# A second buffer for turned tokens, earlier loads, another layout of the norm sums and wide recurrence steps in the SSD units of a hybrid encoder block

## The chip, the core and the metric

The kernel runs on one NeuronCore of a Trainium2 chip, as one launch. The metric is the device time of one execution in microseconds (us); the runs are summed up by their median. The core's engines are TensorE (PE; its weight loads are listed apart as PEld), VectorE (DVE), ScalarE (ACT), GpSimd (POOL) and SyncE (SP), and 16 DMA engines move data between the memory HBM and the on-chip SBUF. TensorE writes to PSUM, a small memory of 8 banks here, which VectorE and ScalarE read.

## The reference

One block on a sequence of 1024 tokens of width 1024. The change lies in the Mamba-2 (SSD) heads: 16 heads of width 64, in two groups, chunks of 128 tokens, both directions.

```python
h = rms_norm(x, norm_mix_pre);  z, xbc, dt_raw, u = split(h @ w_in)
xh, b_ssm, c_ssm = split(silu(conv(xbc)))            # 16 heads of 64; states of 128
# _ssd_scan, once per direction:
scores = einsum("bclgn,bcsgn->bcgls", cc, bc)
y_diag = einsum("bcgrls,bcsgrp->bclgrp", scores[:, :, :, None] * decay, xdt)
states = einsum("bclgn,bcgrl,bclgrp->bcgrpn", bc, decay_to_end, xdt)   # one per chunk
states_in = einsum("bzcgr,bcgrpn->bzgrpn", m, states)                  # decayed sum over earlier chunks
y_off = einsum("bclgn,bcgrpn,bcgrl->bclgrp", cc, states_in, exp(a_cum))
# behind both directions:
y = (y_f + y_b + xh * d_skip) * silu(z)
y_ssd = rms_norm(y, norm_w, per group of 512 channels)
y_s5 = s5_mixer(u)                                   # ends in g * sigmoid(g @ glu_w + glu_b)
x = x + rms_norm(concat(y_ssd, y_s5) @ w_out)
x = x + rms_norm((silu(n @ w_gate) * (n @ w_up)) @ w_down)   # n = rms_norm(x)
```

## The kernel before

The program runs in stages: input projection with the S5 scan (to about 540 us), the SSD units (about 590 to 945 us), the mixing norm, and the feed-forward part (from about 1014 us to the end). All large products are in three float32r terms (high by high, high by low, low by high halves).

**The units.** The work on the 16 heads is cut into eight units of two heads, `unit(q)`, q = 0 to 7; units 0 to 3 are norm group 0, 4 to 7 group 1. They are woven into three other pieces of TensorE work by generators (`fill_with`): the GLU product of the S5 half (line 277, up to about 698 us), the output product of the S5 half (line 1137, `out_s5`) and that of SSD group 0 (line 1137, `out_g0`). A tile scheduler orders each engine's instructions by priorities (`hpri`) and its own costs; the order on each engine is then fixed, and every engine works through its own list in order. SP issues most of the DMAs, and waits in order too.

**One unit.** Four tensors are loaded by `unit_loads(q)`: the two operands `la` and `ra` of the decay exponents (from `na_d` and `rr_d` in HBM) and the tokens `xT`. TensorE turns `xT` (line 871), ScalarE copies the result to `X` (872), VectorE and GpSimd multiply it by the step weights of one direction each to `Xw` (943), and TensorE makes the chunk states from it (956, 28 matmul instructions of 128 columns). The recurrence over chunks stands on VectorE (967): `Sn[step] = Sn[step-1] * cd + state`, six steps with four instructions of 64 columns each, one per direction and head. Then, for each half of the sequence, decays (981 to 989), the masked scores `M` (1002, 1003), the products (1008, 1022) and the sums in `y` (1010 to 1027).

**Its tail.** ScalarE squares `y` (1032 or 1035), VectorE adds the squares to `ssum` (1036), ScalarE and VectorE write `y` as two halves `hl` (1040, 1041), with the tokens ordered by step, and SP stores them to `ch_d` and `cl_d` (1042, 1043). After four units `group_norm` sums `ssum` over the partitions by 16 matmul instructions (1050); in them every weight load reads `ssum` at a distance of 8 elements. The output products load `ch_d` and `cl_d` as `cat` (1127), and `out_g0` adds to partial sums `m` that go through `m_d` (load 1162, sum on VectorE 1166, store 1167; two buffers).

**Before the units**, `dt_prep` makes the step weights `wdt`, the chunk decays `cd`, and the sums' halves `rhl` (858, 859), which GpSimd stores to `rr_d` and `na_d` by eight DMAs (862, 863); `unit_loads(0)` reads them back. `rhl` and `X` share one buffer.

Of the kernel before, what the change touches and what calls it, by code (L numbers as in the profile page):

```python
# [9 lines left out]
F32 = mybir.dt.float32  # L10
F32R = mybir.dt.float32r
I32 = mybir.dt.int32
AF = mybir.ActivationFunctionType
ALU = mybir.AluOpType
PSUM = bass.MemoryType.PSUM
ADD, SUB, MUL = ALU.add, ALU.subtract, ALU.mult
# [116 lines left out]
def hymba_block(ctx, tc, P, out, dbg=None, upto=99):  # L133
# [663 lines left out]
    def dt_prep():  # L797
# [5 lines left out]
        t = ptmp()  # L803
# [30 lines left out]
        t = ptmp()  # L834
# [17 lines left out]
        for d in range(2):  # L852
            pe.matmul(t[:, 128 * d:128 * d + 128], af[:, d].rearrange("p c h -> p (c h)"), (tri_le, tri_ge)[d], start=True, stop=True)
            pe.transpose(t[:, 256 + 128 * d:384 + 128 * d], ln[:, d].rearrange("p c h -> p (c h)"), ident)
        rhl = un.tile([128, 2, 4, 128], F32R, tag="X", name="rhl")
        rh, rl = rhl[:, 0], rhl[:, 1]
        tv = t.rearrange("p (n l) -> p n l", n=4)
        act.copy(rh, tv)
        dve.tensor_tensor(rl, tv, rh.bitcast(F32), op=SUB)
# [71 lines left out]
    def unit(q, ssum):  # L931
        g = q // 4
        with hpri("u1"):
            L, Rr = la[q % 2], ra[q % 2]
            if q not in uts:
                unit_loads(q)
            xT = uts[q]
            X = un.tile([128, 8, 128], F32, tag="X", name="X")
            transposes(X, xT)
            Xw = un.tile([128, 2, 8, 2, 64], F32, tag="Xw", name="Xw")  # L940
            for d in range(2):
                w = wdt[:, :, 16 * d + 2 * q:16 * d + 2 * q + 2].unsqueeze(3).to_broadcast([128, 8, 2, 64])
                pd(f"xw{d}").tensor_tensor(Xw[:, d], X.rearrange("p c (h e) -> p c h e", h=2), w, op=MUL)
            zt = un.tile([128, 1024], F32, tag="zt", name="zt")
            sp.dma_start(zt, z_d[128 * q:128 * q + 128, :])
        yield
        with hpri("u2"):

            Sn = un.tile([128, 2, 7, 128], F32, tag="Sn", name="Sn")
            for s0 in range(0, 7, 2):  # L950
                t = ptmp()
                ns = min(2, 7 - s0)
                for d in range(2):
                    for s in range(ns):
                        c = s0 + s if d == 0 else 7 - s0 - s
                        pe.matmul(t[:, 256 * s + 128 * d:256 * s + 128 * d + 128], Bt[:, c, g, :],  # L956
                                  Xw[:, d, c].rearrange("p h e -> p (h e)"), start=True, stop=True)
                for s in range(ns):
                    st = s0 + s
                    if st == 0:  # L960
                        act.copy(Sn[:, :, 0, :], t[:, 0:256].rearrange("p (d e) -> p d e", d=2))
                        continue
                    for d in range(2):
                        for hh in range(2):
                            es = slice(64 * hh, 64 * hh + 64)
                            o = 256 * s + 128 * d + 64 * hh
                            dve.scalar_tensor_tensor(Sn[:, d, st, es], Sn[:, d, st - 1, es], cd[:, d, st, 2 * q + hh:2 * q + hh + 1],
                                                     t[:, o:o + 64], op0=MUL, op1=ADD)
            if q in KN['cd']:
                conv_silu(*conv_taps(q + 4, None))  # L970
        y = un.tile([128, 1024], F32, tag="yg", name="yg", bufs=2)
        for hf in range(2):
            with hpri("u3"):
                sl = HF[hf]
                rv = Rr[:, 4 * hf:4 * hf + 4, :].rearrange("p c l -> p (c l)")
                Es, EFs = [], []
                for hh in range(2):
                    E = un.tile([128, 2, 512], F32, tag="E", name="E", bufs=2)
                    for d in range(2):
                        xp = ptmp()  # L980
                        pe.matmul(xp, L[:, 4 * d + 2 * hf + hh, :], rv, start=True, stop=False)
                        pe.matmul(xp, idr, neg[:, d].rearrange("p c l -> p (c l)"), start=False, stop=True)
                        act.activation(E[:, d], xp, AF.Exp)
                    Es.append(E)
                for d in range(2):
                    EF = un.tile([128, 512], F32, tag="EF", name="EF", bufs=2)
                    xp = ptmp()
                    pe.matmul(xp, efs[:, d, :], rv, start=True, stop=True)
                    act.activation(EF, xp, AF.Exp)
                    EFs.append(EF)  # L990
                if hf == 1 and q < 7:
                    unit_loads(q + 1)
            yield
            with hpri("u4"):
# [33 lines left out]
            if hf == 0:  # L1028
                yield
        with hpri("u4"):  # L1030
            if q % 4 == 0:
                act.activation(ssum, y, AF.Square)
            else:
                sq = io.tile([128, 1024], F32, tag="io", name="sq")
                act.activation(sq, y, AF.Square)
                pd('ss').tensor_tensor(ssum, ssum, sq, op=ADD)
            hl = un.tile([128, 2, 8, 128], F32R, tag="hl", name="hl")
            w = vec2[:, R_N + q:R_N + q + 1]
            yv = y.rearrange("p (k l) -> p l k", l=8)
            act.activation(hl[:, 0], yv, AF.Copy, scale=w)  # L1040
            dve.scalar_tensor_tensor(hl[:, 1], yv, w, hl.bitcast(F32)[:, 0], op0=MUL, op1=SUB)
            Q[KN["cq"]].dma_start(ch_d[128 * q:128 * q + 128], hl.bitcast(F32)[:, 0])
# [2 lines left out]
    @pri("gn")  # L1045
    def group_norm(g, ssum):
        t = ptmp()
        sv = ssum.rearrange("p (k l) -> p l k", l=8)
        for l in range(8):
            pe.matmul(t[:, l:l + 1], sv[:, l, :], ones[:, 0:1], start=True, stop=True)  # L1050
        rms_scale(t[:, 0:8], rg[:, g, :], 1.0 / 512, 1e-5)
# [917 lines left out]
```

## Time and profile before

| | |
|---|---|
| runs before | median 1693.84 us of 3 (1693.69 to 1709.21) |
| the profiled execution | 1697.36 us, its span on the core 1695.7 us, mean granted TensorE clock 0.963 |
| TensorE, matmul | busy 1557.0 us, 92% of the span |
| VectorE | busy 1252.1 us, 74% |
| ScalarE | busy 728.0 us, 43% |
| GpSimd | busy 537.6 us, 32% |
| DMA | 271.61 MB, 160 GB/s over the span |

The profiled execution is the one that the trace shows; its own time is 0.2% over the median of the runs. A busy share is a mean over stages with different limits. Engines are named by their short names, times are counted from the start of the span, and a line number is one of the kernel before.

### The profile page before, as it was taken

The page shows a single profiled execution, that of the slowest core. Times are in us where ns is not written, and L with a number is a line of the kernel's source. Part 1 is how long each engine was busy: PE and PEld are TensorE (multiplying, and loading weights), DVE is VectorE, ACT ScalarE, POOL GpSimd, SP SyncE. Part 2 cuts the span into 40 slices and gives each one's busy share as a digit, 9 for nine tenths or more (in the row PEclk, how much of TensorE's full clock was granted, in tenths as well). Part 3 has the DMA queues.
Part 4 walks back from the last instruction along what each step waited for, and adds up shares of the span by engine and source line. Part 5 has one row for each costly group of instructions (what it writes and reads, how often), then busy time and mean ns, then how long its engine had stood idle before and what let it go on. Part 6 is the DMA issues. An engine that isn't in the chain of part 4 may idle for free.

```text
span 1695.7 us, 22363 instructions
## 1 busy us (share of the span) xinstructions
PE 1557.0 (92%) x7980; PEld 1270.2 (75%) x7980; DVE 1252.1 (74%) x2022; ACT 728.0 (43%) x1238; POOL 537.6 (32%) x499
## 2 busy tenths in 40 slices
PE   7998999889787879999998997999999999999897
PEld 6777788668675666778787775788888888787686
DVE  7445589999862567887576578788888788669777
ACT  6354632122598445444343277322222232344352
POOL 2111121157121020112111041555555555239512
PEclk9999999989799889999999998999999999999999
DMA  6543343243687748777668892333322221592234
GB/s 182 155 134 107 115 153 124 94 128 98 151 210 191 210 129 273 242 245 244 194 217 267 282 297 72 104 119 122 106 100 94 100 100 56 203 341 71 94 111 175
DMA packets 250003, 271.61 MB, mean 160 GB/s; under 512 B 29387, under 2 KB 190659, under 8 KB 249891
## 3 DMA queue, kind: packets, MB, share of 16 engines
q1 hardware_dynamic: 224515, 215.96, 41.2%
q0 software_dynamic: 12896, 33.83, 6.3%
q10 hardware_dynamic: 12480, 20.39, 3.4%
q8 instruction: 63, 1.03, 0.3%
q14 instruction: 49, 0.40, 0.1%
HBM read 185.23 MB, written 84.84 MB: 159 GB/s over the span
## 4 chain that ended last, share of the span: by engine, by line
PE 39%; DVE 10%; DMA 8%; issue 4%; ACT 3%; POOL 3%; SPq 0%; DVEq 0%; POOLq 0%; ACTq 0%
PE acc L1550 13%; PE ptmp L1550 10%; PE acc L1137 4%; PE ptmp L1856 4%; PE acc L1856 3%; DVE dop L1838 2%; DMA m<-m_d 2%; PE acc L277 1%; PE ptmp L956 1%; POOL wd L1823 1%; DMA m_d<-m 1%; DMA cl_d<-ghl 1%; DVE cacc L724 1%; PE ptmp L1022 1%; DMA graw<-g_d 1%
## 5 line engine op out<-in xcount | busy, mean ns | idle before, releaser
L277 PE MATMUL acc<-hTh,whi 128*128 128x512 f32 (+1 forms) x456 | 179.9, 395 | 8.5 <-ACT whi L267 8.0
L1137 PE MATMUL acc<-ohi,cat 128*128 128x512 f32 x512 | 175.7, 409 | 8.6 <-DMA cat<-ch_d 5.5
L277 PE MATMUL acc<-hTh,wlo 128*128 128x512 f32 (+1 forms) x456 | 179.1, 393 | 2.2 <-POOL wlo L268 2.1
L277 PE MATMUL acc<-hTl,whi 128*128 128x512 f32 (+1 forms) x456 | 179.4, 394 | 0.5 <-DVE hTl L337 0.5
L1533 DVE TENSOR_TENSOR wop<-rawp,wop 128x512 fp32r<-128x512 f32 x120 | 137.7, 1148 | 17.9 <-ACT wop L1532 16.7
L1550 PE MATMUL ptmp<-T,wop 128*128 128x512 f32 x528 | 127.9, 399 | 4.1 <-ACT T L1706 3.7
L1550 PE MATMUL acc<-T,wop 128*128 128x512 f32 x528 | 125.7, 393 | 1.6 <-DVE T L1709 1.5
L1856 PE MATMUL ptmp<-dop 128*128 128x512 f32 x528 | 122.2, 393 | 2.9 <-DVE dop L1838 2.9
L1550 PE MATMUL acc<-B,wop 128*128 128x512 f32 x528 | 124.6, 392 | 0.0
L1137 PEld LDWEIGHTS acc<-ohi,cat 128*128 128x128 f32 x512 | 99.3, 195 | 33.2 <-DVE s L1673 4.4
L1550 PEld LDWEIGHTS ptmp<-T,wop 128*128 128x128 f32 x528 | 101.2, 192 | 27.2 <-ACT T L1706 3.9
L268 POOL TENSOR_TENSOR wlo<-raw,whi 128x1024 fp32r<-128x1024 f32 x20 | 50.3, 2514 | 222.4 <-ACT whi L267 222.4
L1856 PEld LDWEIGHTS ptmp<-dop 128*128 128x128 f32 x528 | 100.2, 190 | 24.2 <-DVE dop L1838 3.2
L1550 PEld LDWEIGHTS acc<-T,wop 128*128 128x128 f32 x528 | 98.8, 188 | 24.9 <-DVE T L1709 3.3
L1550 PEld LDWEIGHTS acc<-B,wop 128*128 128x128 f32 x528 | 99.1, 188 | 21.7 <-DVE B L1709 0.2
L277 PEld LDWEIGHTS acc<-hTh,whi 128*128 128x128 f32 x456 | 87.1, 191 | 27.0 <-ACT whi L267 8.4
L1565 ACT ACTIVATE cg<-cg 128x512 f32<-128x512 f32 x44 | 27.8, 633 | 183.0 <-DVE cg L1563 182.9
L1838 DVE TENSOR_TENSOR dop<-da,dop 128x512 fp32r<-128x512 f32 x77 | 76.9, 999 | 36.7 <-ACT dop L1837 36.7
L1571 POOL TENSOR_TENSOR cg<-cg 128x512 f32<-128x512 f32 x44 | 61.8, 1405 | 130.5 <-DVE cg L1566 129.8
L277 PEld LDWEIGHTS acc<-hTh,wlo 128*128 128x128 f32 x456 | 87.1, 191 | 21.5 <-POOL wlo L268 4.1
L1532 ACT CAST wop<-rawp 128x512 fp32r<-128x512 f32 x120 | 70.2, 615 | 76.7 <-POOL rawp L1507 51.2
L1137 PE MATMUL acc<-olo,cat 128*128 128x512 f32 x256 | 103.1, 403 | 0.0
(362 smaller groups left out, 3566.1 us busy)
## 6 DMA issues: line engine op xcount, KB each, us to landing
ff_d<-cg POOLq DMA_DIRECT2D x77, 256.0 KB, 2.3
da<-ff_d SPq DMA_DIRECT2D x35, 512.0 KB
raw<-in_w_in_dram SPq DMA_DIRECT2D x28, 512.0 KB
cat<-ch_d SPq DMA_DIRECT2D x48, 256.0 KB
cat<-cl_d SPq DMA_DIRECT2D x48, 256.0 KB
wd<-in_w_down_dram SPq DMA_DIRECT2D x44, 256.0 KB
rawp<-in_w_gate_dram SPq DMA_DIRECT2D x10, 1024.0 KB
rawp<-in_w_up_dram SPq DMA_DIRECT2D x10, 1024.0 KB
```

Source lines behind the costliest of these rows:

```text
L268: (pool if ("0" if j < 2 else "A" if j < XBC0 else "X" if j < Z0 else "Z" if j < GL0 else "G" if j < FF0 else "F") in KN['pl'] else dve).t ...
L277: pe.matmul(ps, a[:, k, :], b[:, k, sl], start=(k == 0 and n == 0), stop=(k == 7 and n == 2))
L724: (pool if ct in KN['pc'] and k in KN['pk'] else dve).scalar_tensor_tensor(a[:, d], xp[:, r], w[k], a[:, d], op0=MUL, op1=ADD)
L956: pe.matmul(t[:, 256 * s + 128 * d:256 * s + 128 * d + 128], Bt[:, c, g, :], Xw[:, d, c].rearrange("p h e -> p (h e)"), start=True, stop=True)
L1137: pe.matmul(ps, c[:, a, k % 4, :], b[:, k % 2, :], start=(k == 0 and n == 0), stop=(k == n_ - 1 and n == 2))
L1532: act.copy(t[:, 0], src)
L1533: dve.tensor_tensor(t[:, 1], src, t.bitcast(F32)[:, 0], op=SUB)
L1550: pe.matmul(ps, a[:, ai, k, :], b[:, bi, k, :], start=(k == 0 and q == 0), stop=(k == 3 and q == 2))
L1565: act.activation(cg[:, 0], cg[:, 0], AF.Silu)
L1571: pool.tensor_tensor(dst, a, b, op=op)
L1838: dve.tensor_tensor(t[:, k, 1], src, t.bitcast(F32)[:, k, 0], op=SUB)
L1856: pe.matmul(ps, t[:, 0, a, 128 * j:128 * j + 128], t[:, 1, b, :], start=(q == 0 and n == 0), stop=(q == NP - 1 and n == 2))
```

## The change

Five edits in `dt_prep`, `unit` and `group_norm`:

1. `X` has two buffers of its own tag.
2. `rhl` leaves that tag and takes the buffer of `hl`, which the first unit's tail is the next to use.
3. `unit_loads(q + 1)` is written in the first half of unit q, not in the second.
4. The squares are written by step: the activation reads `y` at a distance of 8 elements, as the one for `hl` does, and writes in a row; `ssum` is then in the order in which `group_norm` loads it.
5. A step of the recurrence is two instructions of 256 columns in the place of four of 64: a product of two SBUF operands (the decays broadcast), and a sum with the state in PSUM.

```diff
--- before.py
+++ after.py
@@ -852,8 +852,8 @@
         for d in range(2):
             pe.matmul(t[:, 128 * d:128 * d + 128], af[:, d].rearrange("p c h -> p (c h)"), (tri_le, tri_ge)[d], start=True, stop=True)
             pe.transpose(t[:, 256 + 128 * d:384 + 128 * d], ln[:, d].rearrange("p c h -> p (c h)"), ident)
-        rhl = un.tile([128, 2, 4, 128], F32R, tag="X", name="rhl")
-        rh, rl = rhl[:, 0], rhl[:, 1]
+        rhl = un.tile([128, 2, 8, 128], F32R, tag="hl", name="rhl")
+        rh, rl = rhl[:, 0, 0:4], rhl[:, 1, 0:4]
         tv = t.rearrange("p (n l) -> p n l", n=4)
         act.copy(rh, tv)
         dve.tensor_tensor(rl, tv, rh.bitcast(F32), op=SUB)
@@ -935,7 +935,7 @@
             if q not in uts:
                 unit_loads(q)
             xT = uts[q]
-            X = un.tile([128, 8, 128], F32, tag="X", name="X")
+            X = un.tile([128, 8, 128], F32, tag="X", name="X", bufs=2)
             transposes(X, xT)
             Xw = un.tile([128, 2, 8, 2, 64], F32, tag="Xw", name="Xw")
             for d in range(2):
@@ -960,12 +960,9 @@
                     if st == 0:
                         act.copy(Sn[:, :, 0, :], t[:, 0:256].rearrange("p (d e) -> p d e", d=2))
                         continue
-                    for d in range(2):
-                        for hh in range(2):
-                            es = slice(64 * hh, 64 * hh + 64)
-                            o = 256 * s + 128 * d + 64 * hh
-                            dve.scalar_tensor_tensor(Sn[:, d, st, es], Sn[:, d, st - 1, es], cd[:, d, st, 2 * q + hh:2 * q + hh + 1],
-                                                     t[:, o:o + 64], op0=MUL, op1=ADD)
+                    hv = [Sn[:, :, i, :].rearrange("p d (h e) -> p d h e", h=2) for i in (st - 1, st)]
+                    dve.tensor_tensor(hv[1], hv[0], cd[:, :, st, 2 * q:2 * q + 2].unsqueeze(3).to_broadcast([128, 2, 2, 64]), op=MUL)
+                    dve.tensor_tensor(hv[1], hv[1], t[:, 256 * s:256 * s + 256].rearrange("p (d h e) -> p d h e", d=2, h=2), op=ADD)
             if q in KN['cd']:
                 conv_silu(*conv_taps(q + 4, None))
         y = un.tile([128, 1024], F32, tag="yg", name="yg", bufs=2)
@@ -988,7 +985,7 @@
                     pe.matmul(xp, efs[:, d, :], rv, start=True, stop=True)
                     act.activation(EF, xp, AF.Exp)
                     EFs.append(EF)
-                if hf == 1 and q < 7:
+                if hf == 0 and q < 7:
                     unit_loads(q + 1)
             yield
             with hpri("u4"):
@@ -1028,15 +1025,16 @@
             if hf == 0:
                 yield
         with hpri("u4"):
+
+            yv = y.rearrange("p (k l) -> p l k", l=8)
             if q % 4 == 0:
-                act.activation(ssum, y, AF.Square)
+                act.activation(ssum.rearrange("p (l k) -> p l k", l=8), yv, AF.Square)
             else:
                 sq = io.tile([128, 1024], F32, tag="io", name="sq")
-                act.activation(sq, y, AF.Square)
+                act.activation(sq.rearrange("p (l k) -> p l k", l=8), yv, AF.Square)
                 pd('ss').tensor_tensor(ssum, ssum, sq, op=ADD)
             hl = un.tile([128, 2, 8, 128], F32R, tag="hl", name="hl")
             w = vec2[:, R_N + q:R_N + q + 1]
-            yv = y.rearrange("p (k l) -> p l k", l=8)
             act.activation(hl[:, 0], yv, AF.Copy, scale=w)
             dve.scalar_tensor_tensor(hl[:, 1], yv, w, hl.bitcast(F32)[:, 0], op0=MUL, op1=SUB)
             Q[KN["cq"]].dma_start(ch_d[128 * q:128 * q + 128], hl.bitcast(F32)[:, 0])
@@ -1045,7 +1043,7 @@
     @pri("gn")
     def group_norm(g, ssum):
         t = ptmp()
-        sv = ssum.rearrange("p (k l) -> p l k", l=8)
+        sv = ssum.rearrange("p (l k) -> p l k", l=8)
         for l in range(8):
             pe.matmul(t[:, l:l + 1], sv[:, l, :], ones[:, 0:1], start=True, stop=True)
         rms_scale(t[:, 0:8], rg[:, g, :], 1.0 / 512, 1e-5)
```

Since a scheduler sets the order, instructions move too. On GpSimd, at the stores of the sums' halves (`rr_d`, `na_d`) that stand ahead of the first unit:

```order
 L908 MEMSET efs 128x256
 L862 DMA rr_d<-rhl 8x16x128
+L943 TENSOR_TENSOR Xw<-X,wdt 128x1024
 L863 DMA na_d<-rhl 2x64x128
 L862 DMA rr_d<-rhl 8x16x128
```

The first unit's product `Xw` on GpSimd moved ahead of seven of the eight stores; it stood behind the last of them. On ScalarE the two copies to `X` of that unit (872) moved likewise, from behind the cast to `rhl` to a place ahead of the copy to `ac` (838), which the step weights and `rhl` need; on VectorE its `Xw` now stands right behind the second half of `rhl`, and on TensorE its 28 matmul instructions of line 956 stand 22 rows of line 277 earlier, with 25 such rows between them and the first of line 981.

On SP in `out_g0`, where `m0` is the partial sum that is loaded, added to and stored (before):

```order
L1099 DMA oraw_8087<-in_w_out_dram 128x2x512
L1127 DMA cat_7818<-cl_d_66 128x4x128
L1167 DMA m_d_67<-m0_7726 128x512
L1099 DMA oraw_8093<-in_w_out_dram 128x2x512
L1127 DMA cat_7888<-ch_d_65 128x4x128
L1162 DMA m0_7796<-m_d_67 128x512
L1167 DMA m_d_67<-m0_7746 128x512
L1127 DMA cat_7888<-cl_d_66 128x4x128
L1127 DMA cat_7926<-ch_d_65 128x4x128
L1127 DMA cat_7926<-cl_d_66 128x4x128
L1167 DMA m_d_67<-m0_7796 128x512
L1162 DMA m0_7816<-m_d_67 128x512
```

and now:

```order
L1097 DMA oraw_7997<-in_w_out_dram 128x2x512
L1165 DMA m_d_67<-m0_7646 128x512
L1125 DMA cat_7804<-ch_d_65 128x4x128
L1125 DMA cat_7804<-cl_d_66 128x4x128
L1125 DMA cat_7842<-ch_d_65 128x4x128
L1165 DMA m_d_67<-m0_7666 128x512
L1160 DMA m0_7712<-m_d_67 128x512
L1125 DMA cat_7842<-cl_d_66 128x4x128
L1125 DMA cat_7862<-ch_d_65 128x4x128
L1160 DMA m0_7732<-m_d_67 128x512
L1125 DMA cat_7862<-cl_d_66 128x4x128
L1165 DMA m_d_67<-m0_7712 128x512
```

The load of the fourth partial sum (7816, now 7732) stood behind the store of the third (7796) and stands ahead of it now (7712).

On SP at the tail of unit 4, where `hl` are the halves of `y` and `cat` what the output product of the S5 half loads (before):

```order
L945 DMA zt_7288<-z_d_62 128x1024
L1042 DMA ch_d_65<-hl_7233 128x1024
L1127 DMA cat_7425<-ch_d_65 128x4x128
L1127 DMA cat_7425<-cl_d_66 128x4x128
L1127 DMA cat_7428<-ch_d_65 128x4x128
L1127 DMA cat_7428<-cl_d_66 128x4x128
L1043 DMA cl_d_66<-hl_7233 128x1024
L1127 DMA cat_7527<-ch_d_65 128x4x128
```

and now:

```order
L945 DMA zt_7228<-z_d_62 128x1024
L1040 DMA ch_d_65<-hl_7173 128x1024
L1041 DMA cl_d_66<-hl_7173 128x1024
L1125 DMA cat_7357<-ch_d_65 128x4x128
L1125 DMA cat_7357<-cl_d_66 128x4x128
L1125 DMA cat_7360<-ch_d_65 128x4x128
L1125 DMA cat_7360<-cl_d_66 128x4x128
L1125 DMA cat_7455<-ch_d_65 128x4x128
```

The store to `cl_d` moved ahead of four loads of `cat`; in unit 5 it did the same. From unit 3 on the loads of `la`, `ra` and `xT` stand at the same places among their neighbours as before, and so do the turns (871), the copies to `X` and the products `Xw`.

## Rows read from the trace of the kernel before

**Rows 1.** The page, part 1: busy time, share of the span, instructions.
```profile
PE 1557.0 (92%) x7980; PEld 1270.2 (75%) x7980; DVE 1252.1 (74%) x2022; ACT 728.0 (43%) x1238; POOL 537.6 (32%) x499
```

**Rows 2.** Waits by engine and line, TensorE, 590 to 1014: total, times, longest.
```profile
PE ptmp L956 <- DVE Xw L943: 18.8, 7, 8.4
```

**Rows 3.** Timeline of TensorE at the first unit: start, us, instruction, idle before.
```profile
613.58 1.19 PE L956 MATMUL ptmp<-Xw,Bt 128*128 128x128 f32 x4 [8.38 <-DVE Xw L943]
615.25 4.55 PE L956 MATMUL ptmp<-Xw,Bt 128*128 128x128 f32 x24 [0.48 <-POOL Xw L943]
...
619.87 0.40 PE L981 MATMUL ptmp<-ra,la 128*128 128x512 f32 x1
```

**Rows 4.** Windows, 606 to 620: length, busy by engine, granted clock, DMA share, GB/s.
```profile
606.00:620.00 14.00, 5.94 (x30) 5.63 (x31) 7.32 (x17) 4.54 (x7) 2.94 (x1) 0.63 0.33 99
```

**Rows 5.** Timeline of ScalarE at the same place.
```profile
611.10 1.07 ACT L872 COPY X<-ptmp 128x512 f32<-128x512 f32 x2 [10.06 <-DMA na_d<-rhl]
```

**Rows 6.** Timeline of GpSimd at the same place (its DMA issues included).
```profile
598.09 0.61 POOL L862 DMA_DIRECT2D rr_d<-rhl  x1 [37.94 <-ACT rhl L858]
...
602.83 0.80 POOL L863 DMA_DIRECT2D na_d<-rhl  x1
612.26 2.94 POOL L943 TENSOR_TENSOR Xw<-X,wdt 128x1024 f32<-128x1024 f32 x1 [8.63 <-ACT X L872]
```

**Rows 7.** Timeline of SyncE's queue at the same place.
```profile
611.09 0.29 SPq L923 DMA_DIRECT2D la<-na_d  x1
```

**Rows 8.** The tensor na_d: its four stores, issue to landing.
```profile
DMA to landing us min/median/max: 4.3/6.4/8.2
```

**Rows 9.** Timeline of TensorE: the group norms, and unit starts after and without one.
```profile
796.11 4.93 PE L956 MATMUL ptmp<-Xw,Bt 128*128 128x128 f32 x28
...
828.18 3.36 PE L956 MATMUL ptmp<-Xw,Bt 128*128 128x128 f32 x28 [1.37 <-DVE Xw L943]
...
946.42 3.75 PE L1050 MATMUL ptmp<-ones,ssum 128*128 128x1 f32 x16
```

**Rows 10.** Windows around the two group norms (columns as in rows 4).
```profile
790.00:802.00 12.00, 11.66 (x54) 10.97 (x54) 6.78 (x20) 2.71 (x5) 4.57 (x2) 0.72 0.93 285
946.00:960.00 14.00, 12.28 (x45) 10.42 (x44) 4.61 (x6) 2.10 (x2) 1.66 (x1) 0.76 0.86 270
```

**Rows 11.** Timeline of VectorE: dependent adds of 256, and the recurrence of unit 0.
```profile
584.61 0.88 DVE L827 SCALAR_TENSOR_TENSOR e<-e,z 128x256 f32<-128x256 f32 x2
...
618.22 3.92 DVE L967 SCALAR_TENSOR_TENSOR Sn<-Sn,cd,ptmp 128x64 f32<-128x64 f32 x20 [0.45 <-PE ptmp L956]
```

**Rows 12.** Groups by line, ScalarE: count, busy us, mean ns, idle before.
```profile
L1040 ACT ACTIVATE hl<-yg,vec 128x1024 fp32r<-128x1024 f32 x8 | 18.2, 2279 | 0.0
...
L1035 ACT ACTIVATE sq<-yg 128x1024 f32<-128x1024 f32 x6 | 6.4, 1060 | 21.8 <-DVE yg L1027 21.8
```

**Rows 13.** The chain that ended last, 870 to 900: start, us, what.
```profile
880.89 2.42 DMA m<-m_d
...
893.66 0.33 SPq L1167
...
894.08 4.67 DMA m<-m_d
```

**Rows 14.** Timeline of VectorE and TensorE at the start of the last unit.
```profile
900.14 1.22 DVE L943 TENSOR_TENSOR Xw<-X,wdt 128x1024 f32<-128x1024 f32 x1
...
901.50 4.99 PE L956 MATMUL ptmp<-Xw,Bt 128*128 128x128 f32 x28 [4.23 <-DVE Xw L943]
```

**Rows 15.** Timeline of GpSimd and VectorE: the two products of a unit side by side.
```profile
747.80 1.92 POOL L943 TENSOR_TENSOR Xw<-X,wdt 128x1024 f32<-128x1024 f32 x1 [8.61 <-ACT X L872]
...
748.08 2.73 DVE L943 TENSOR_TENSOR Xw<-X,wdt 128x1024 f32<-128x1024 f32 x1
```

**Rows 16.** Timeline of SyncE's queue in unit 4.
```profile
833.25 0.39 SPq L1127 DMA_DIRECT2D cat<-ch_d  x1
...
837.57 0.33 SPq L1043 DMA_DIRECT2D cl_d<-hl  x1
```

## The prediction

> **What bounds the kernel now.** I read the page's busy shares first: TensorE is busy for 92% of the span, VectorE for 74%, ScalarE for 43% [rows 1]. So a microsecond is won only where TensorE idles, runs at a low clock, or takes longer over an instruction than the same work takes elsewhere. The change touches the unit stage alone, so the second view is TensorE's waits between 590 and 1014 us. The largest group there is the chunk states waiting for VectorE's `Xw`: 18.8 us in 7 waits, the longest of them 8.4 [rows 2]. The timelines around that longest wait, at the first unit, come third, and the two group norms fourth. [...] Around the norms the clock is 0.72 and 0.76 with a busy TensorE [rows 10], and the norm's one-column instructions take 3.75 us for 16 [rows 9]. All sums are made on the profiled execution's 1697.36 us and carried to the median of the runs by 1693.84/1697.36, 0.2% less. A change of less than 1%, 17 us, can hardly be told from none by a measurement of this kernel.
>
> **First unit.** ScalarE's copies to `X` wait 10.06 us for the last store of `na_d` to land, because `X` takes over `rhl`'s buffer [rows 5]. Edits 1 and 2 end that. What is late next decides the gain. The decay matmuls of line 981 need `la`, which SP issues when `na_d` has landed: at 611.09 [rows 7]. The order shows that this gets later for two reasons. The two copies to `X` (1.07 for both, rows 5) now stand ahead of work that `rhl` needs on ScalarE, and GpSimd's `Xw` stands ahead of seven of the eight stores, whose issues begin at 598.09 and end at 603.63 [rows 6]. `Xw` on GpSimd takes 2.94 in that place [rows 6] and 1.92 elsewhere [rows 15]; I take 2.94. So `na_d` lands at 611.09 + 1.07 + 2.94 = 615.1. The load of `la` is not in the rows; the nearest prices are 2.42 for a load on SP [rows 13] and 4.3 for the fastest store of `na_d` [rows 8]; I take the middle, 3.36. Line 981 then begins at 618.46, against 619.87 now [rows 3]: 1.41 earlier, and two more instructions of line 277 are done by then, 0.23 each from the starts in the trace's order, 0.46. **Term: -1.9.** With 1.92 and 2.42 it is -3.8, with 2.94 and 4.3 -0.9; the last landing, 7.46 behind the issue's end now, may lie between 4.3 and 8.2 [rows 8], which takes the bounds to -7.0 and -0.2. So the wait isn't removed, it moves from `Xw` to `la`: TensorE does its states and the 25 rows of line 277 early, and then stands before line 981 instead. The clock falls there as it does now, and the 2.4 us lost to it (5.74 less 3.36) are not credited.
>
> **Group norms.** The strided weight loads go. Now an instruction takes 3.75/16 = 0.234 us [rows 9]; the nearest row for one with a dense weight load of that size is line 956, 3.36/28 = 0.12 [rows 9]. 16 x 0.114 = 1.8, twice: **-3.6**, all of it on TensorE's own time. Beyond it, the clock at these places: 12 us at 0.72 and 14 us at 0.76 [rows 10] lose 3.4 each against full speed; unit 4's states right behind the first norm take 4.93 for unit 5's 3.36 [rows 9]. In front of the drop stand the norm's instructions, which fill the engine's time with little work; if they are half as long, the drop may be absent or the same. I take half of 6.8: **-3.4**, bounds 0 and -6.8.
>
> **Partial sums.** In `out_g0` the load of the fourth `m` waits in SP's list behind the store of the third: store issued at 893.66, load at 894.08, and 4.67 us until it lands [rows 13], where a load of the same size alone takes 2.42. VectorE's `Xw` of the last unit stands behind that sum and starts at 900.14, and TensorE waits 4.23 for it [rows 14]. The load moves ahead of that store, by one queue entry of 0.4 us and part of the 2.25 that it lands late: **-1.0**, bounds 0 and -4.2.
>
> **What it costs.** Unit 0 shows a step of the recurrence at 3.92/20 = 0.196 us an instruction; 24 of them are 4.7 us a unit. Twelve dependent instructions of 256 columns cost 0.88/2 = 0.44 each by the two at 584.61 [rows 11], together 5.3: +0.6 a unit on VectorE. [...] The squares take 1.06 now; read at a distance of 8 elements, like line 1040, they take 2.28 [rows 12]: +1.22 on ScalarE in each of 8 tails. In all 8 x (0.6 + 1.22) = 14.6 us of work on engines with room; `hl` is written behind it, one unit or more ahead of who reads it. Only at the last unit is no later unit's work left to cover it, where the norm waits for the squares and the output product for `cat`: 0.6 + 1.22 = 1.8, and 0.7 for places in between where TensorE waits for `M`: **+2.5**, bounds 0 and 14.6.
>
> **SP at the tails of units 4 and 5.** The store to `cl_d` is moved ahead of four `cat` loads. SP works in order, and the store waits for VectorE's half of `hl`: it was issued at 837.57, the first `cat` load at 833.25 [rows 16]. With the squares' 1.22 those four loads come up to 4.32 + 1.22 = 5.5 us later. The output products that read them hold two steps of `cat` in advance; this is the cover, and if it is gone, TensorE waits up to 5.5 in each. **+1.0**, bounds 0 and 11.
>
> **At nothing:** the loads of edit 3 and the second `X` from unit 3 on. The order leaves `la`, `ra`, `xT`, the turns and both `Xw` where they were among their neighbours, so the other six waits of rows 2 remain, but for the 1.0 above.
>
> **Sum:** -1.9 - 3.6 - 3.4 - 1.0 + 2.5 + 1.0 = -6.4, so 1691.0 for the profiled execution and **1687.4** as a median. With the terms' bounds, of which not all fall on one side, this case lies between 1681 and 1692.
>
> **Rivals.**
> *The stall is gone and the clock stays up.* If `la` lands before TensorE has done its 25 rows of line 277, the first unit gives 8.38 + 0.48 + 2.4 = 11.3, and with the whole 6.8 of the norms: -11.3 - 3.6 - 6.8 - 1.0 + 2.5 + 1.0 = -19.2, 1674.7. For it: the wait for `X` is the only one that the trace shows there. Against it: `na_d` lands late even now, and two things are put ahead of it.
>
> *The layout and the new home do next to nothing.* The first unit gains 0.2, the clock falls as before: -0.2 - 3.6 - 1.0 + 2.5 + 1.0 = -1.3, 1692.5. Against it: the slower norm instructions have no other visible reason than their stride.
>
> *Slower: the `cl_d` store ahead of the `cat` loads.* If the loads are not covered in units 1, 4 and 5, where an output product runs, each costs 5.5: 16.5 + 2.5 - 9.9 = +9.1, 1702.9. It decides from the point where a `cat` load lands after TensorE has finished the step before it. For it: a `cat` buffer has little depth, and TensorE hardly idles there now, so every wait would be new. Against it: two steps in advance are more than 5.5 us.
>
> *VectorE behind GpSimd.* The side-by-side products show 2.73 for VectorE's `Xw` [rows 15] against 1.22 alone [rows 14]. The recurrence's new product reads two SBUF operands too, 48 times in all; the old form read PSUM. GpSimd is busy for 32% [rows 1]; 48 x 0.32 x 1.5 (the 2.73 less 1.22) = 23 us more on VectorE, and with half of it on the path -6.4 + 11.5 = +5.1, 1698.9. [...] Against its size: after `Xw`, GpSimd has little to do while the states are made.
>
> **How the numbers follow.** Chances: the forecast 0.50, the next-to-nothing rival 0.22, the full gain 0.10, the `cat` loads 0.13, GpSimd 0.05. The range runs from 1675 to 1700: it leaves out part of the full gain and most of the `cat` case, which has a tail on both sides. Faster by over 1% (under 1676.9) is most of the full gain and the forecast's lower tail, 0.09; slower by over 1% (over 1710.8) needs the `cat` case at more than its price, 0.04; within 1%, 0.87.
>
> **What would show it.** In the changed profile: ScalarE's copies to `X` without the 10 us wait; GpSimd's `Xw` ahead of the `na_d` stores, SP's issue of `la` near 615, and a TensorE wait of some 7 us before line 978 (981 before). The norm's instructions near 0.12 each, and a clock above 0.72 and 0.76 around them. Steps of the recurrence near 0.9 for two instructions, squares at 2.28, no new wait for `cat` in units 1, 4 and 5, and a shorter wait than 4.23 at the last unit. I am wrong if `la` is issued early after all, if `cat` waits appear, or if the time moves outside the unit stage.

## The result and the profile after

The changed kernel takes 1707.5 us in the median of 20 runs (1699.89 to 1716.5), the kernel before 1697.73 in 20 runs beside it; the ratio is 1.0055, 95% interval 1.0039 to 1.0071. It is slower by 0.55%, where 0.4% faster was forecast. Of the 20 us between the forecast, 1687.4, and the 1707.5, 3.9 are the base: the forecast stands on a median of three runs of the kernel before, 1693.84. The profiled execution's span is 1701.7 us at a mean clock of 0.965. TensorE is busy for 1552.5 us, 4.5 less than before, and the span is 6.0 longer: it waits more.

Where the time went is read by stage. In both traces I count from TensorE's last transposition of `ln` (line 854; at 594.84 before, 592.70 now), which lies just ahead of the units. What lies ahead of it and behind the output products is the same code, and differs by some us from one profiled execution to the next (behind: 681.7 to 686.7 in the fourteen profiles of this study). In TensorE's order line 854 itself moved a little: in the kernels with the buffers 1498 instructions of line 277 lie ahead of it, in the others 1494, so that all columns but that of e3 show 0.9 us too much of a gain (four at 0.23 each). The table gives, for the starts of the chunk states of some units and for the end of the last output product, how much later (+) or earlier (-) than before they come, in us; its other columns are the experiments below. Each column is one execution.

| | after | e1 | e2 | e3 | e4 | e5 | e6 | e12 |
|---|---|---|---|---|---|---|---|---|
| unit 0 | -11.6 | -11.7 | -11.5 | 0.0 | -11.7 | -11.7 | -11.6 | -11.7 |
| unit 1 | -5.5 | -5.5 | -5.0 | -4.7 | -5.8 | -5.0 | -5.2 | -4.1 |
| unit 5 | -7.2 | -3.3 | -7.9 | -2.7 | -4.2 | -2.9 | -7.2 | -7.7 |
| unit 6 | -3.3 | -3.3 | -5.0 | +0.1 | -4.2 | -2.0 | -7.2 | -7.6 |
| unit 7 | +3.6 | -4.0 | -1.5 | +4.9 | -4.5 | +1.7 | -5.7 | -7.4 |
| end of products | +3.9 | -0.5 | -1.0 | +6.3 | -4.0 | +4.8 | -4.8 | -4.5 |

The gain at unit 0 is in good part order alone: 22 instructions of line 277, some 5 us, stood ahead of its states and stand behind them now (44 lay between line 854 and the states, now 18 do, and four moved ahead of line 854). By unit 2 the order of this work is the old one again. So the changed kernel is ahead as far as unit 5, loses 10.8 us from there to unit 7, and never gets it back. TensorE's waits of the changed kernel, 590 to 1014 (us in all, times, longest), name the new ones:

```profile
PE ptmp L956 <- DVE Xw L943: 10.1, 7, 2.7
PE acc L1135 <- DMA cat<-ch_d: 9.2, 4, 4.1
PE ptmp L978 <- DVE Sn L965: 7.3, 6, 2.1
PE ptmp L871 <- DVE yg L1007: 3.5, 1, 3.5
PE ptmp L985 <- DVE Sn L965: 2.7, 3, 1.4
```

The first line answers to [rows 2]: 18.8 are 10.1 now, and the longest is 2.7. But `Sn`, the recurrence, for which TensorE waited nowhere before, costs 7.3 + 2.7 = 10.0 in 9 waits, `yg` 3.5, and `cat` 9.2 where it was 5.5. Seven of the nine waits for `Sn`, 8.0 us of the 10.0, and the one for `yg` lie in units 5 to 7.

The clock has its part too. Units 5 and 6, first before, then now (length, busy by engine from TensorE on, granted clock, DMA share, GB/s):

```profile
828.18:860.55 32.37, 30.99 (x188) 25.90 (x189) 20.79 (x44) 12.98 (x20) 6.16 (x4) 1.00 0.60 189
860.55:901.50 40.95, 36.69 (x211) 30.25 (x212) 27.22 (x52) 16.00 (x23) 7.31 (x4) 1.00 0.82 256
```

```profile
818.84:855.07 36.23, 31.74 (x188) 25.61 (x189) 21.78 (x32) 14.38 (x20) 5.51 (x4) 1.00 0.53 169
855.07:902.95 47.88, 41.33 (x211) 33.17 (x211) 28.45 (x40) 17.72 (x23) 6.59 (x4) 0.89 0.72 224
```

TensorE does the same number of instructions in 10.8 us more. Half of that, 5.4, is idle time. The other half is instructions that take longer. In unit 6 the granted clock falls to 0.50 from 864.6 to 871.4, amid TensorE's waits of 1.61 and 0.97 for `Sn`, and again from 898.7 to 902.2, behind its wait for `yg`; the second fall has its counterpart before at 901.9 (0.51 from there to 904), just behind the start of unit 7. The first has none: over the first 34 to 35 us of unit 6 the clock is 0.90 in the changed kernel, 0.95 in e2 and e3, and 1.00 in the kernel before, e1, e4, e5, e6 and e12. The three that lose clock there are those with `hl` between the steps of the wide form. Over the whole of 590 to 1014 the changed kernel's mean clock is the better one, 0.97 against 0.95, so that what it loses there in all is waiting.

Here is VectorE's timeline in unit 5, first before, then now:

```profile
830.67 4.69 DVE L967 SCALAR_TENSOR_TENSOR Sn<-Sn,cd,ptmp 128x64 f32<-128x64 f32 x24 [1.45 <-ACT Sn L961]
835.27 2.26 DVE L1041 SCALAR_TENSOR_TENSOR hl<-yg,vec,hl 128x1024 fp32r<-128x1024 f32 x1
```

```profile
822.33 0.43 DVE L964 TENSOR_TENSOR Sn<-Sn,cd 128x256 f32<-128x256 f32 x1 [2.45 <-ACT Sn L961]
822.86 0.42 DVE L965 TENSOR_TENSOR Sn<-Sn,ptmp 128x256 f32<-128x256 f32 x1
823.32 0.42 DVE L964 TENSOR_TENSOR Sn<-Sn,cd 128x256 f32<-128x256 f32 x1
824.63 2.21 DVE L1039 SCALAR_TENSOR_TENSOR hl<-yg,vec,hl 128x1024 fp32r<-128x1024 f32 x1 [0.89 <-ACT hl L1038]
826.73 0.44 DVE L965 TENSOR_TENSOR Sn<-Sn,ptmp 128x256 f32<-128x256 f32 x1
...
830.02 1.18 DVE L964 TENSOR_TENSOR Sn<-Sn,cd 128x256 f32<-128x256 f32 x1
831.31 0.42 DVE L965 TENSOR_TENSOR Sn<-Sn,ptmp 128x256 f32<-128x256 f32 x1
```

Before, the 24 instructions of the recurrence ran in one piece, 4.69 us, and the second half of `hl` came behind them. Now the recurrence lasts from 822.33 to 831.73, 9.4 us, though eleven of its twelve instructions take 0.42 to 0.44 each, and one 1.18. Between the third and the fourth stands `hl` of the unit before, 2.21 us, and ahead of it VectorE stands still for 0.89, because ScalarE is not done with the first half. The states' sums in PSUM come free that much later, and TensorE, which needs a free place for the decay products, stands:

```profile
828.23 0.47 PE L978 MATMUL ptmp<-ra,la 128*128 128x512 f32 x1 [2.11 <-DVE Sn L965]
```

The order of VectorE's list says the same of other units: `hl` stands between the steps in units 2, 3, 5, 6 and 7, and in unit 7 a sum of squares and two partial sums `m` besides; in the kernel before, that is so in unit 7 alone, with a sum and `hl`. Other work stands between the steps of units 0 to 3 too, in the kernel before of units 1 to 3.

### The profile page after: what moved, and what is told of

It is laid out like the page before. It is cut to its first block, busy times and chain, and to the rows that moved or that the text cites. A ratio compares the mean times of both kernels' runs of the same rounds, so it can differ in the third digit from the quotient of the medians.

```text
span 1701.7 us, 22248 instructions
## 1 busy us (share of the span) xinstructions
PE 1552.5 (91%) x7980; PEld 1261.9 (74%) x7980; DVE 1253.1 (74%) x1926; ACT 740.3 (44%) x1238; POOL 539.9 (32%) x499
```

## The experiments

The theories, as they stood when the runs were made. **W**: the wide form loses because other VectorE work, `hl` above all, now stands between its steps. **D**: it loses as a chain of twelve dependent instructions, whatever stands between. **N**: the longer squares are the loss. **E**: the earlier unit loads are. **F**: it lies outside the units. **M**: the order of the partial sums' loads on SP. All ratios are to the kernel before, on the same chip.

**e1, e2: the changed kernel without one edit.** In e1 the recurrence is the old one:

```diff
-  dve.tensor_tensor(hv[1], hv[0], cd[...].to_broadcast([128, 2, 2, 64]), op=MUL)
-  dve.tensor_tensor(hv[1], hv[1], t[:, 256 * s:256 * s + 256]..., op=ADD)
+  for d in range(2):
+      for hh in range(2):
+          dve.scalar_tensor_tensor(Sn[:, d, st, es], Sn[:, d, st - 1, es], cd[...], t[:, o:o + 64], op0=MUL, op1=ADD)
```

> The changed kernel with the recurrence as it was (four instructions of 64 columns a step); the other four edits stay. Theory W (in the wide form the scheduler puts other VectorE work, above all the 2.2 us second half of hl, which itself waits for ScalarE, between the dependent steps, so PSUM comes free late and TensorE waits for Sn): the Sn waits, 10.0 us in 9 in the changed kernel, are gone, the first unit's gain stays, ratio to the kernel before 0.993 to 0.997. Rival N (the longer squares delay the tails): they are still in, ratio 1.002 to 1.006. Rival F (the loss lies outside the unit stage, in other buffer places and the feed-forward part): ratio 1.002 to 1.006.

Measured: 1.0014 (0.9996 to 1.0032). Without the wide form 0.41 points less, and TensorE's waits for `Sn` are 1.4 in the place of 10.0. W's range missed, though, as did the others' (1.0014 lies between them): something else in it still eats the first unit's gain.

In e2 the squares and `ssum` have the old layout:

```diff
-  act.activation(sq.rearrange("p (l k) -> p l k", l=8), yv, AF.Square)
+  act.activation(sq, y, AF.Square)
-  sv = ssum.rearrange("p (l k) -> p l k", l=8)
+  sv = ssum.rearrange("p (k l) -> p l k", l=8)
```

> The changed kernel with the squares and norm sums in their old layout; the wide recurrence stays. Theory W: hl stands between the steps of the recurrence still, only its wait for ScalarE is about 1.1 us shorter in units 5 to 7; Sn waits 5 to 9 us, group norm slower by 3.6 again: ratio 1.002 to 1.007. Rival N: ratio 0.993 to 0.998. Rival F: 1.002 to 1.006, with Sn waits unimportant.

Measured: 1.0019 (0.9995 to 1.0043), waits for `Sn` 5.3. That is just under W's range and 0.36 points less than the changed kernel, so that edit 4 costs too. N alone is out, since the rest is not back.

**e3, e4: one edit alone.** The wide recurrence (edit 5's lines in the kernel before), and the buffers (edits 1 and 2).

> The kernel before with the wide recurrence alone. Theory W: Sn waits of 5 to 10 us appear in units 3 to 7 and nothing is gained at the first unit: ratio 1.004 to 1.010, the slowest of the four. Rival N: no change, 0.999 to 1.002. Rival F: no change, 0.999 to 1.002, since no buffer moves.

> The kernel before with the second buffer of X and the other home of the sums' halves alone. Theory W: the first unit's stall of 8.9 us is down to about 4 (waits of 2.7 and 1.7 as in the changed kernel) and the clock stays up, nothing is lost: ratio 0.993 to 0.997. Rival F: the moved buffers cost more than the stall gives, ratio 1.000 to 1.005.

Measured: e3 1.0028 (1.0009 to 1.0047), waits for `Sn` 7.4; slower, as W says, by less than it said. e4 0.9973 (0.9951 to 0.9996): faster, though just short of W's range, and F is out, since its buffers moved. TensorE at the first unit of e4:

```profile
608.00 3.36 PE L956 MATMUL ptmp<-Xw,Bt 128*128 128x128 f32 x28 [2.67 <-DVE Xw L943]
...
619.05 0.47 PE L981 MATMUL ptmp<-ra,la 128*128 128x512 f32 x1 [2.64 <-DMA la<-na_d]
```

The stall of 8.9 us has become two, 2.67 for `Xw` and 2.64 for `la`, and here the clock is 1.00 from 600.9 to 610.9 and the states take 3.36. Little of it is left at unit 1. Of the 5.8 in the table 0.9 are the place of line 854, and some 2.8 are order: 12 instructions of line 277 that stood ahead of that point before are still to come. TensorE's waits from line 854 to unit 1 add up to 7.8 us, 10.9 before, because a new one, of 2.54 for `M`, has come in; and the granted clock from 625.9 to 651.9 is 0.93, where it was 1.00 over the same stretch before. In all of e4's units TensorE's waits for `M` are:

```profile
PE ptmp L1008 <- DVE M L1003: 5.1, 4, 2.5
```

It was 1.3 before. That VectorE as a whole sets the time there is not shown: in the kernel before it is busy for 22.32 of the 26 us from 619.8 to 645.8, and TensorE for 24.00.

**e5, e6: hl queued behind the recurrence.** The last write of `hl` (and the store to `cl_d`) is held back until the next unit's recurrence is written, and put behind its last instruction on VectorE:

```diff
-  dve.scalar_tensor_tensor(hl[:, 1], yv, w, ...)
-  Q[KN["cq"]].dma_start(cl_d[...], hl.bitcast(F32)[:, 1])
+  def finish():   # the two lines above; kept in pend, of unit 7 called at once
...
+  if pend:        # in the next unit, behind its recurrence; last: its last instruction
+      with hpri("u4"), tc.issue_after(last.ins):
+          pend.pop()()
```

> The changed kernel, all five edits, but the second half of hl on VectorE (and its store to cl_d) is queued behind the last step of the next unit's recurrence, so that it stands no longer between the steps. Theory W (the wide form's loss is hl between the steps): the Sn waits, 10.0 us in the changed kernel, fall below 3, and some 5 us come back: ratio to the kernel before 1.000 to 1.003. Rival D (the wide form loses by being a dependent chain of twelve, whatever stands between): Sn waits and time stay, 1.004 to 1.007. Rival N (squares): 1.004 to 1.007, since their delay stays.

> The kernel before with X's second buffer, the other home of the sums' halves and the wide recurrence, hl behind the recurrence as in the run before; squares and the place of the unit loads as before. Theory W: the first unit's gain (ratio 0.997 alone) stays and the wide form costs nothing or gives 1 to 2 us: 0.995 to 0.998. Rival D: 0.999 to 1.002.

Measured: e5, with all five edits, 1.0014 (0.9992 to 1.0037), as good as e1 without the wide form. e6 0.9983 (0.9959 to 1.0007), just above W's range and below D's. VectorE in unit 5 of e5, and TensorE's waits for `Sn`:

```profile
830.88 0.43 DVE L966 TENSOR_TENSOR Sn<-Sn,cd 128x256 f32<-128x256 f32 x1 [2.46 <-ACT Sn L963]
...
836.20 0.42 DVE L967 TENSOR_TENSOR Sn<-Sn,ptmp 128x256 f32<-128x256 f32 x1
836.54 2.70 DVE L1045 SCALAR_TENSOR_TENSOR hl<-yg,vec,hl 128x1024 fp32r<-128x1024 f32 x1
```

```profile
PE ptmp L983 <- DVE Sn L967: 2.9, 3, 2.0
...
PE ptmp L990 <- DVE Sn L967: 1.0, 1, 1.0
```

In units 4 to 6 of e5 nothing stands between the twelve steps any more; in unit 5 they run in one piece, 830.88 to 836.62, 5.74 us. That is 1.05 longer than the 24 were, and without `hl` between them it costs nothing that can be measured (e6 against e4, +0.10 points; e12 against e10, +0.03; e5 against e1, none; each uncertain by some 0.3). D is out. The waits are 3.9, where under 3 was expected; but for that W holds. In units 0 to 3 other work still stands between the steps (in unit 3 of e5 they take 13.64 us), and no loss is seen from it. No run has `hl` queued behind the old recurrence alone. There is little for it to move there: in the kernel before `hl` stands between the steps of unit 7 alone, in e1, e4 and e10 of unit 1 too.

**e7, e8: the other single edits.** The unit loads half a unit earlier (`hf == 1` becomes `hf == 0`), and edit 4 by itself.

> The kernel before with the unit loads written half a unit earlier, alone. The loads of la and ra pass stores and cat loads on SP's queue in units 2 and 3. All theories: little, ratio 0.999 to 1.002; above 1.002 would make it a cause of its own (a rival E: stores and cat loads come later behind the unit loads).

> The kernel before with the squares and norm sums kept by step, alone. Theory W: the group norms win 3.6 us and the 1.1 us longer squares delay hl without standing between the steps in units 3 to 6: ratio 0.998 to 1.001. Rival N: the longer squares cost more than the norms give whatever the recurrence's form, 1.002 to 1.004.

Measured: e7 0.9992 (0.9968 to 1.0016), nothing; E is out. e8 1.0027 (1.0006 to 1.0048): edit 4 loses by itself, as N says. In e8's trace the gain is plain, and so is what takes it:

```profile
950.79 1.84 PE L1050 MATMUL ptmp<-ones,ssum 128*128 128x1 f32 x16
957.48 0.80 PE L1137 MATMUL acc<-ohi,cat 128*128 128x512 f32 x1 [4.84 <-DVE m L1166]
```

The norm's 16 instructions take 1.84 and not 3.75, and behind them TensorE waits 4.84 for the partial sum, where it was 1.73.

**e11: the long squares without the norm.** The squares are read and written at a distance of 8 elements; `ssum` and the norm stay.

```diff
-  act.activation(sq, y, AF.Square)
+  act.activation(sq.rearrange("p (k l) -> p l k", l=8), yv, AF.Square)
```

> The kernel before with the squares read (and written) at a distance of 8 elements, so that they take some 2.1 us and not 1.06, while the sums and the group norm keep their old layout. Rival N (the longer squares are what the fourth edit costs): 1.002 to 1.005, no better than the fourth edit alone (1.0027). If the squares are hidden: 0.999 to 1.001, and the loss of the fourth edit lies elsewhere, in the norm itself.

Measured: 1.0021 (0.9998 to 1.0044). The squares by themselves cost about what edit 4 costs; the interval just reaches no change. How they cost is seen on VectorE: the sum over squares waits for them. Its group in the kernel before, with that of `hl`, then the changed kernel's, then e11's (count, busy us, mean ns, idle ahead and for whom):

```profile
L1041 DVE SCALAR_TENSOR_TENSOR hl<-yg,vec,hl 128x1024 fp32r<-128x1024 f32 x8 | 18.1, 2261 | 3.9 <-issue 2.9 <-ACT hl L1040 1.0
...
L1036 DVE TENSOR_TENSOR ssum<-ssum,sq 128x1024 f32<-128x1024 f32 x6 | 7.3, 1222 | 2.7 <-ACT sq L1035 2.6
```

```profile
L1039 DVE SCALAR_TENSOR_TENSOR hl<-yg,vec,hl 128x1024 fp32r<-128x1024 f32 x8 | 18.5, 2311 | 8.4 <-ACT hl L1038 5.8 <-issue 2.6
...
L1035 DVE TENSOR_TENSOR ssum<-ssum,sq 128x1024 f32<-128x1024 f32 x6 | 7.4, 1226 | 8.2 <-ACT sq L1034 8.2
```

```profile
L1037 DVE TENSOR_TENSOR ssum<-ssum,sq 128x1024 f32<-128x1024 f32 x6 | 7.3, 1223 | 7.6 <-ACT sq L1036 7.6
```

2.7 us of standing still become 8.2 and 7.6 with the long squares. In all five kernels with the long ones they are 6.5 to 8.2, in all nine with the short ones 2.4 to 2.9.

**e9, e10, e12: what is left.** e9 is e6 with the old recurrence in units 6 and 7 (`if q < 6:` ahead of the wide lines); e10 has edits 1 to 3; e12 is the changed kernel without edit 4 and with `hl` behind the recurrence, as in e5.

> As the run with home, wide recurrence and hl behind it, but units 6 and 7 keep the narrow recurrence. Theory M (in the wide form SP's order in out_g0 changes: the third partial sum's load stands behind the second's store and further cat loads, so the sum on VectorE is some 3 us later and yg, and TensorE's turns of the last unit, wait behind it): with the narrow form in units 6 and 7 the order of these loads is the old one, the wait of TensorE for yg, 3.0 us, is gone, and the gain of the wide form in units 2 to 6 stays to the end: ratio to the kernel before 0.994 to 0.997. Rival: the wide form's early gain is only waited off later in any case, 0.997 to 0.999, as with home alone.

> The kernel before with X's second buffer, the other home of the sums' halves and the earlier unit loads. Sum of the single effects 0.9973 and 0.9992: 0.995 to 0.998 if they add up; 0.998 to 1.001 if the earlier loads cost something beside the earlier first unit (rival E).

> The changed kernel without the fourth edit and with hl queued behind the recurrence: home, earlier loads, wide recurrence. If both causes are real and add up (hl between the steps 0.4%, the fourth edit 0.3%): 0.997 to 1.000. Theory M says not below that, since the order of the partial sums' loads is the one of the wide form.

Measured: e9 0.9976 (0.9955 to 0.9998), e10 0.9973 (0.9952 to 0.9994), e12 0.9976 (0.9953 to 0.9999). e9 has no wait for `yg`, but the products end no earlier: a wait of 3.5 for the next stage's `mix` and other waits take its place, so M names a wait and no loss. e10 is no faster than e4. e12 is 0.43 points under e2, and 0.38 under e5. The five that keep the buffers, leave out edit 4 and have no `hl` between wide steps (e4, e6, e9, e10, e12) lie at 0.9973 to 0.9983, below both kernels, though e6's interval reaches the kernel before; which is best can't be told.

**The account, in points of per cent.** `hl` between the steps: 0.41 (changed kernel against e5) and 0.43 (e2 against e12). The wide form with `hl` between its steps: 0.41 (changed kernel against e1), 0.46 (e2 against e10), 0.28 alone. Edit 4: 0.36 (changed kernel against e2), 0.38 (e5 against e12), 0.41 (e1 against e10), 0.27 alone. The buffers: -0.27. Earlier loads: -0.08 alone, none beside the buffers. Each figure is uncertain by some 0.2 to 0.3, but the two costs repeat in pairs of different runs. That 0.42 + 0.38 - 0.27 = 0.53 comes near the 0.55 of the whole is no further test, since the same runs stand on both sides. The ratios decide, not the ends of single profiles: e5's profiled execution took 1707.44 us, 5.2 over its median, the changed kernel's 1703.66, 3.8 under its own, so that the last row of the table, later for e5 than for the changed kernel, decides nothing between them.

## Why the prediction was wrong, step by step

**First unit: the place was right, the size was not.** The stall moved to `la` as forecast, but the first decay product is 7.1 earlier from line 854 (6.2 without the place of that line), where 1.4 was taken, with 0.5 for two instructions of line 277, and 7.0 was the bound. The clock stayed up in this profile: 1.00 from 598.5 to 612.5, 0.63 in [rows 4], and the states take 3.36 and not the 1.19 + 4.55 = 5.74 of [rows 3]. That is no firm gain: of the nine kernels with the buffers six show 3.36 there, and e2, e5 and e6 5.0, at a clock of 0.83 over the 10 us around them.

```profile
599.80 3.36 PE L956 MATMUL ptmp<-Xw,Bt 128*128 128x128 f32 x28 [2.69 <-DVE Xw L943]
...
610.62 0.47 PE L978 MATMUL ptmp<-ra,la 128*128 128x512 f32 x1 [1.72 <-DMA la<-na_d]
```

Several prices were too high. GpSimd's `Xw` took 1.92, not 2.94, and ScalarE had room for the copies, so the issues end at 603.48, 10.8 after line 854, where 8.8 was before: 2.0 later and not 4.0.

```profile
596.01 0.61 POOL L862 DMA_DIRECT2D rr_d<-rhl  x1 [37.91 <-ACT rhl L858]
596.64 1.92 POOL L943 TENSOR_TENSOR Xw<-X,wdt 128x1024 f32<-128x1024 f32 x1
...
602.68 0.80 POOL L863 DMA_DIRECT2D na_d<-rhl  x1
```

And `na_d` lands faster: the slowest of the four took 5.7, it was 8.2 [rows 8], so that `la` is issued 4.95 behind the end of the last issue, where 7.46 was taken. The load of `la` itself let TensorE go on 2.2 behind its issue, and not 3.36.

```profile
DMA to landing us min/median/max: 3.7/4.8/5.7
```

```profile
608.43 0.69 SPq L923 DMA_DIRECT2D la<-na_d  x2
```

The 1.4 taken and these three (2.0, 2.5 and 1.2) are the 7.1.

What is left at the end is 4.6 us (0.27%, between 0.04 and 0.49) in e4, with these edits alone: more than the term, less than the 7.1. In e4's profile a part came back as the wait for `M` and as lower clock. The term counted `la` alone as the wait that comes next.

**Group norms and the clock around them: right in the trace, and worth nothing.** The instructions take 1.62 for 14 and 1.84 for 16, 0.115 to 0.116 each; in this profile the clock is 1.00 around the first norm and still 0.76 behind the second [rows 9, 10], half of 6.8 as taken:

```profile
783.24 1.62 PE L1048 MATMUL ptmp<-ones,ssum 128*128 128x1 f32 x14
...
787.27 3.36 PE L956 MATMUL ptmp<-Xw,Bt 128*128 128x128 f32 x28 [1.14 <-DVE Xw L943]
...
948.95 1.84 PE L1048 MATMUL ptmp<-ones,ssum 128*128 128x1 f32 x16
954.92 0.80 PE L1135 MATMUL acc<-ohi,cat 128*128 128x512 f32 x1 [4.12 <-DMA cat<-ch_d]
```

```profile
780.00:796.00 16.00, 13.89 (x83) 11.13 (x84) 12.81 (x19) 8.06 (x13) 6.05 (x3) 1.00 0.98 297
946.00:960.00 14.00, 9.34 (x38) 7.76 (x39) 4.76 (x6) 1.51 (x2) 1.66 (x1) 0.76 0.81 279
```

At the first norm this is not sure either: in the ten kernels with the old norm the clock fell at its end or just behind it (to 0.50 from 793 to 798 in the kernel before; in e4, e11 and e12 it is 0.79, 0.68 and 0.79 over the 7 or 8 us behind the norm); with the new one it stayed up in e1 and e8 too (1.00 from 787 to 808 in e8), and fell in e5 (0.66 from 795 to 802), where unit 4's states take 5.94. And the two rows with a bracket show that it is paid back, in part or in whole: unit 4 waits 1.14 for `Xw`, and behind the second norm TensorE waits 4.12 for `cat`, where it waited 1.73 for `m`. e8, which has the faster norms, is no better than e11, which has not (1.0027 and 1.0021).

**Partial sums: half of it was overlooked.** I read that the fourth load had moved ahead of a store, and VectorE's wait for it fell from 3.99 to 1.13. I did not read that the third had moved behind one, though the order shows it. SP issues it at 892.83, in the kernel before at 889.71:

```profile
889.60 1.41 SPq L1165 DMA_DIRECT2D m_d<-m  x1
892.83 0.33 SPq L1160 DMA_DIRECT2D m<-m_d  x1
```

VectorE stands 8.07 for it, where it stood 4.01, with `yg` behind, and TensorE for `yg`; VectorE's row before comes first:

```profile
892.88 0.75 DVE L1166 SCALAR_TENSOR_TENSOR m<-acc,rg,m 128x512 f32<-128x512 f32 x1 [4.01 <-DMA m<-m_d]
```

```profile
896.48 0.75 DVE L1164 SCALAR_TENSOR_TENSOR m<-acc,rg,m 128x512 f32<-128x512 f32 x1 [8.07 <-DMA m<-m_d]
897.14 0.74 DVE L1007 SCALAR_TENSOR_TENSOR yg<-xT,dvec,ptmp 128x512 f32<-128x512 f32 x1
```

```profile
897.94 0.66 PE L871 MATMUL ptmp<-ident,xT 128*128 128x128 f32 x4 [3.48 <-DVE yg L1007]
```

Both waits together are 9.2, where they were 8.0. TensorE's wait at the last unit has changed its name more than its size: 3.48 for `yg` and 0.49 for `Xw`, where it was 4.23 for `Xw` [rows 14]. e9 shows that without the wait for `yg` others come, so that it is no loss of its own.

**What it costs: this step failed.** It priced the instructions and not their order. The prices were right: 0.42 for a step's instruction (0.44 taken), 2.15 for the squares (2.28 taken). What failed is the reason that this is work on engines with room, and that `hl` is written ahead of who reads it. It was not the reader of `hl` that waited: VectorE works in order (in unit 5 the sum at 826.73 had its product from 823.74 and the states from 822.2 on, and came only behind `hl`, its 2.21 and the 0.89 ahead of it), so `hl`, with its wait for ScalarE, is a wait of the recurrence if it stands between two steps, and the sum over squares holds up whatever stands behind it. In place of +2.5 for both, `hl` between the steps costs 0.42% (7 us), in idle time and in clock, and edit 4, its gain already taken off, 0.27 to 0.41% (5 to 7 us). VectorE's list, which is fixed ahead of the run, could have told it: `hl` stands there between two steps in five units. The prediction read the orders of the other engines, and of VectorE's none but the place of `Xw`.

**SP at the tails: the order was right, and the +1.0 cost nothing.** The `cat` loads of unit 4 come behind the store to `cl_d`, at 827.29, and TensorE waits for none of them until 946.

```profile
824.57 0.32 SPq L1040 DMA_DIRECT2D ch_d<-hl  x1
826.87 0.32 SPq L1041 DMA_DIRECT2D cl_d<-hl  x1
827.29 0.41 SPq L1125 DMA_DIRECT2D cat<-ch_d  x1
```

**The rivals.** The slower one that I priced, the `cat` loads of units 1, 4 and 5, did not happen. The one with VectorE behind GpSimd did, in small: the product at 830.02 took 1.18, beside `M` on GpSimd (1.28 from 829.64 on), but the mean of all 48 is 0.465 against 0.418 for the sums, 2.3 us in all. No rival named what happened, a long instruction of VectorE's own between two steps of a chain on it. And the sentence that a change of less than 1% can hardly be told from none was too cautious: with 20 runs each 0.55% is told, with 0.16 to either side.

**Open:** by which waits edit 4's loss reaches the end. They differ from kernel to kernel (`m` in e8, `cat` and `Sn` in the changed kernel); that VectorE's standing ahead of the sums is their common source is suggested by its going with the squares in every kernel, and not shown, as no run has long squares and no such standing. What stands behind the longer squares on ScalarE comes later as well: in unit 5 the copy of the first state starts right behind them in both kernels, and the recurrence stands 2.45 for it now and 1.45 before; no run tells the two apart. Open too is how `hl`'s cost divides between idle time and clock: the halves above are those of one execution.

## What to carry to other kernels

Fewer, wider instructions can be a loss if they turn partly independent steps into a dependent chain: 0.28 to 0.46% in these runs with `hl` between the steps, and nothing that could be measured without. Here the scheduler put other work between the links (why it did is not shown; a gap that it saw there is a guess), and a long piece of it, with what that waited for, became part of the chain. Before a change is priced by its instructions, look in the order of the engine that it stands on for what has come between them; if it must not be there, queue it behind the last step. And a wait of the busiest engine that goes away is worth only what the next waits, and the clock, leave of it: 8.9 us of stall gave 4.6.

## What the runs showed of the hardware

Reads at a distance of 8 elements (32 bytes) took about twice as long as reads in a row, on two engines: the squares of 128x1024 took ScalarE 2.15 and not 1.06 us, and one of the norm's instructions, a weight load with one column, took TensorE 0.234 and not 0.115. Why is not shown. Of the first unit's two products `Xw`, side by side in both kernels, one kept its usual time and the other took longer, but not the same one: 1.23 on VectorE and 2.94 on GpSimd before, 3.29 and 1.92 now. That is why the price from [rows 6] did not hold.
